# First half of the second layer's modulation moved to the head of the first layer's expert stage

## The chip, the cores and the metric

The kernel runs on one core of a Trainium2 chip. The metric is the device time of one execution in microseconds (us). Times below are counted from the start of the profiled span. The engines are TensorE (PE; PEld is its loading of weights), VectorE (DVE), ScalarE (ACT), GpSimd (POOL) and SyncE (SP). SyncE and GpSimd issue the transfers (DMAs); all of them run on the same 16 DMA engines, SyncE's in the queue that the profile calls q1 and GpSimd's in q0. An engine takes its instructions in the order in which they stand, and a wait holds up what is behind it.

## The reference

Two layers work on 1024 latent tokens and 256 context tokens, each of width 1024 in float32. A layer mixes tokens (two convolutions, windowed and global attention), then runs 16 experts of which each takes its best 128 latent tokens (and 32 context tokens, in the first layer only). Both parts are modulated by a vector that comes from the conditioning `c` alone:

```
mods = silu(c) @ ada_w[i] + ada_b[i]                 # 6 x 1024 values: sh1, sc1, g1, sh2, sc2, g2
h = rms_norm(x, n1) * (1 + sc1) + sh1                # input of the mixers
x_new = x + g1 * (mixers(h) @ w_out)
h2 = rms_norm(x_new, n2) * (1 + sc2) + sh2           # input of the experts
x_new = x_new + g2 * expert_choice_ffn(h2, ...)
# expert_choice_ffn: gates, idx = top_k(softmax(h2 @ router)); rows h2[idx];
# y = (silu(rows @ w_gate) * (rows @ w_up)) @ w_down; added back to rows idx with the gates
```

`ada_w[i]` is 1024 x 6144. It depends on no token, so layer 2's modulation can be computed at any time before layer 2.

## The kernel before

**Precision.** Every large product is made of three matmuls (`mm3`, L272 to L274) on a high and a low part of both sides. Weights are split as they arrive: ScalarE rounds a half chunk to its high part `wh` (L110), VectorE subtracts to get the low part `wl` (L111). There are five `wh` and five `wl` buffers in the first layer's expert stage.

**The expert stage (`moe`).** For each expert, gate, up and down weights come as four chunks of 128 x 4 x 512 floats (1 MiB, tile `rw`, L1188). The chunks go through a ring of 11 buffers (`raw`, made of two pools of 6 and 5), strictly in turn: a chunk that is asked for earlier takes the earlier buffer, whoever asks. The rows of an expert are gathered by an indirect transfer (`xs`, L1262), transposed on TensorE (`pt`, L1250) and split; gate and up products go to `pm`, their product is transposed, multiplied by down weights, scaled by the gate values and the modulation row `g2b`, and scattered with addition into `xacc` (L1343). The context's share of an expert is small matmuls straight from `rw` (L1235); a chunk's buffer is free once both have read it.

**The head of the stage.** The projection before it ends with the router's logits; `topk_x` finds the 128 best tokens of all 16 experts on VectorE (L1115 to L1118), turns the table over on TensorE (L1132, L1134) and writes `idx` (L1141). The gather of expert 0 needs `idx`. While the top-k runs, SyncE already asks for expert 0's weights: the four gate chunks and two up chunks. The other two up chunks and three gate chunks of expert 1 are issued by GpSimd, behind the gathers.

**The modulation.** One modulation step (`ada_mm`, L168) loads one 1 MiB chunk of `ada_w` into the same ring (`rw`, L171) and makes 16 small matmuls with the conditioning as the stationary side (`pc` from `rw` and `cT`, L174). `ada0(l, ...)` is the first third of the modulation (sh1 and sc1) in eight steps. After the fourth and the eighth it adds the bias tile `abias` (`mt`, L190), transposes the sum on TensorE (two transposes, L193) and writes `modT` (L196, L198). The bias tile is first cleared by VectorE (L160) and then filled by two small transfers (L165). `ada(l, 1, ...)` is the second third (g1 and sh2), eight steps again, then one addition and a store to `mods` (L211, L216). `moe` chains the two generators for layer 2 into `nxt`, and `pump(nxt, n)` runs `n` steps of it. Before the change the only places are one step in each of experts 1 to 10 and whatever is left (six steps) after the loop. So "first half" in the title is the eight steps of `ada0`. The last third (`raw`, L171) is made in layer 2's front.

**Order.** The program is written in this order, and a scheduler then moves instructions within their dependences; the order on each engine is fixed before the kernel runs.

Of the kernel before, what the change touches and what calls it, by code (L numbers as in the profile page):

```python
# [51 lines left out]
class Trunk:  # L52
# [1091 lines left out]
    def moe(self, l):  # L1144
# [6 lines left out]
        with ExitStack() as st:  # L1151
# [108 lines left out]
            def fetch(e):  # L1260
                xs = wk.tile([128, D], F32, name="xs")
                self.ga_mark = nc.gpsimd.indirect_dma_start(out=xs, out_offset=None, in_=self.h2[l],  # L1262
                                             in_offset=bass.IndirectOffsetOnAxis(ap=idx[:, e:e + 1], axis=0))
                return xs, fetch_c(e) if CTX and e else None

            def fetch_c(e):
                xc = wc.tile([64, 512], F32, name="xc")
                nc.gpsimd.indirect_dma_start(out=xc, out_offset=None, in_=hv,
                                             in_offset=bass.IndirectOffsetOnAxis(ap=idc[:, e:e + 1], axis=0))
                return xc  # L1270
# [81 lines left out]
            nxt = iter(())  # L1352
            if l + 1 < self.layers:
                stage = (raw.tile([128, 4, 512], F32, name="rw", tag="raw") for _ in itertools.count())
                nxt = itertools.chain(self.ada0(l + 1, stage, mp, _Renamed(psc), pst),
                                      self.ada(l + 1, 1, stage, 4, mp, _Renamed(psc)))
            last, xg = l + 1 == self.layers, None
            x = fetch(0)
            ga0 = self.ga_mark
            X = gather(0, x)  # L1360
# [148 lines left out]
```

## Time and profile before

| what | value |
|---|---|
| median of 3 runs | 2796.9 us (2791.25 to 2802.22) |
| the profiled execution, its own time | 2792.68 us |
| its span | 2790.9 us |
| TensorE busy in the span | 2564.8 us, 92% |
| VectorE, ScalarE, GpSimd busy | 2073.6, 1553.0 and 397.9 us |
| moved from and to memory | 594.44 MB, 213 GB/s on average |
| granted clock of TensorE over the span | 0.968 of full speed |
| top-k at the head of the first expert stage | 704.75 to 742.2 us |
| first matmul of expert 0 | 749.72 us |

The profiled execution is 4.2 us below the median. A row of the trace has the start, the duration, the engine, the line of the kernel, the operation and its tiles, and in brackets how long the engine sat idle before it and what ended that.

### The profile page before, as it was taken

The page shows a single profiled execution, that of the slowest core. Times are in us where ns is not written, and L with a number is a line of the kernel's source. Part 1 is how long each engine was busy: PE and PEld are TensorE (multiplying, and loading weights), DVE is VectorE, ACT ScalarE, POOL GpSimd, SP SyncE. Part 2 cuts the span into 40 slices and gives each one's busy share as a digit, 9 for nine tenths or more (in the row PEclk, how much of TensorE's full clock was granted, in tenths as well). Part 3 has the DMA queues.
Part 4 walks back from the last instruction along what each step waited for, and adds up shares of the span by engine and source line. Part 5 has one row for each costly group of instructions (what it writes and reads, how often), then busy time and mean ns, then how long its engine had stood idle before and what let it go on. Part 6 is the DMA issues. An engine that isn't in the chain of part 4 may idle for free.

```text
span 2790.9 us, 44135 instructions
## 1 busy us (share of the span) xinstructions
PE 2564.8 (92%) x17043; PEld 2033.0 (73%) x17043; DVE 2073.6 (74%) x3076; ACT 1553.0 (56%) x2255; POOL 397.9 (14%) x713
## 2 busy tenths in 40 slices
PE   6999988999799999999998899989996699999994
PEld 5898777877566666666665699777875588887783
DVE  4368866765877777777775558776766899989896
ACT  5212366743366666666664622466632588887774
POOL 1152000000520111111100142100001011111111
PEclk8999999999899999999999899999998899999998
DMA  6345100133689898989886442300048699999995
GB/s 239 115 133 179 57 9 16 33 113 127 240 294 318 295 318 290 330 289 326 276 302 225 135 146 79 98 9 9 9 171 297 249 369 377 377 376 377 376 339 203
DMA packets 297819, 594.44 MB, mean 213 GB/s; under 512 B 20446, under 2 KB 47560, under 8 KB 297608
## 3 DMA queue, kind: packets, MB, share of 16 engines
q1 hardware_dynamic: 275288, 515.58, 52.1%
q0 software_dynamic: 22320, 76.03, 9.0%
q8 instruction: 134, 2.20, 0.3%
q14 instruction: 77, 0.63, 0.1%
HBM read 541.16 MB, written 50.40 MB: 212 GB/s over the span
## 4 chain that ended last, share of the span: by engine, by line
PE 74%; issue 9%; DVE 6%; DMA 5%; ACT 4%; POOL 1%; SPq 0%; POOLq 0%; ACTq 0%; DVEq 0%
PE pm L273 10%; PE pm L272 10%; PE pm L274 10%; PE mm L272 6%; PE mm L274 5%; PE mm L273 5%; PE pc L1235 4%; PE pb L881 4%; PE po L272 2%; PE po L273 2%; PE po L274 2%; PE pb L864 2%; PE pt L1250 2%; PE Sx L793 1%; PE Sl L793 1%
## 5 line engine op out<-in xcount | busy, mean ns | idle before, releaser
L111 DVE TENSOR_TENSOR wl<-rw,wh 128x1024 fp32r<-128x1024 f32 x762 | 908.6, 1220 | 126.3 <-ACT wh L110 102.6
L110 ACT ACTIVATE wh<-rw 128x1024 fp32r<-128x1024 f32 x762 | 794.6, 1059 | 230.8 <-PE pm L274 186.8
L273 PE MATMUL pm<-wl,xh 128*128 128x512 f32 x1024 | 410.4, 401 | 3.4 <-DVE wl L111 2.3
L274 PE MATMUL pm<-wh,xl 128*128 128x512 f32 x1024 | 400.2, 391 | 0.0
L272 PE MATMUL pm<-wh,xh 128*128 128x512 f32 x1024 | 399.7, 395 | 0.0
L272 PEld LDWEIGHTS pm<-wh,xh 128*128 128x128 f32 x1024 | 193.1, 189 | 54.2 <-issue 12.6
L273 PEld LDWEIGHTS pm<-wl,xh 128*128 128x128 f32 x1024 | 192.9, 188 | 51.1 <-DVE wl L111 9.1
L274 PEld LDWEIGHTS pm<-wh,xl 128*128 128x128 f32 x1024 | 193.0, 188 | 37.4
L272 PE MATMUL pm<-wh,hh 128*128 128x512 f32 x512 | 202.0, 397 | 9.5 <-ACT wh L110 9.5
L273 PE MATMUL pm<-wl,hh 128*128 128x512 f32 x512 | 203.9, 398 | 6.3 <-DVE wl L111 6.3
L274 PE MATMUL pm<-wh,hl 128*128 128x512 f32 x512 | 201.7, 394 | 0.0
L1343 POOL DMA_INDIRECT xacc<-y,idx x31 | 86.8, 2799 | 647.2 <-DVE y L1330 647.2
L548 DVE SCALAR_TENSOR_TENSOR yab<-u,pT,yab 128x1295 f32<-128x1295 f32 (+1 forms) x120 | 166.4, 1419 | 0.2
L272 PE MATMUL mm<-wh,hh 128*128 128x256 f32 x512 | 145.7, 286 | 4.3 <-ACT cd L456 3.6
L273 PE MATMUL mm<-wl,hh 128*128 128x256 f32 x512 | 144.0, 282 | 0.0
L274 PE MATMUL mm<-wh,hl 128*128 128x256 f32 x512 | 143.9, 281 | 0.0
L274 PE MATMUL mm<-hh,wl 128*128 128x512 f32 x320 | 126.0, 399 | 0.0
L273 PE MATMUL mm<-hl,wh 128*128 128x512 f32 x320 | 125.5, 398 | 0.0
L272 PE MATMUL mm<-hh,wh 128*128 128x512 f32 x320 | 124.9, 406 | 0.0
L110 ACT ACTIVATE wh<-wr 128x512 fp32r<-128x512 f32 x72 | 45.1, 628 | 141.8 <-DMA wr<-in_w_in_dram 71.8
L272 PEld LDWEIGHTS pm<-wh,hh 128*128 128x128 f32 x512 | 96.6, 189 | 29.9 <-ACT wh L110 10.5
L273 PEld LDWEIGHTS pm<-wl,hh 128*128 128x128 f32 x512 | 96.6, 189 | 29.4 <-DVE wl L111 10.2
(406 smaller groups left out, 5172.4 us busy)
## 6 DMA issues: line engine op xcount, KB each, us to landing
rw<-in_w_down_dram SPq DMA_DIRECT2D x127, 1024.0 KB
rw<-in_w_up_dram SPq DMA_DIRECT2D x125, 1024.0 KB
rw<-in_w_gate_dram SPq DMA_DIRECT2D x123, 1024.0 KB
raw<-in_ada_w_dram SPq DMA_DIRECT2D x48, 512.0 KB
wr<-in_w_in_dram SPq DMA_DIRECT2D x72, 256.0 KB
rw<-in_ada_w_dram SPq DMA_DIRECT2D x16, 1024.0 KB
xt<-in_x_dram SPq DMA_DIRECT2D x16, 512.0 KB
wr<-in_w_out_dram SPq DMA_DIRECT2D x16, 512.0 KB
```

Of the source, the lines that this page charges most:

```text
L110: a = self.nc.scalar.activation(hi, src, AF.Copy)
L111: self.mark = self.nc.vector.tensor_sub(lo, src, hi.bitcast(F32))
L272: nc.tensor.matmul(p, lh, rh, start=first, stop=False)
L273: nc.tensor.matmul(p, lh, rl, start=False, stop=False)
L274: self.pe_mark = nc.tensor.matmul(p, ll, rh, start=False, stop=last)
L548: nc.vector.scalar_tensor_tensor(o, x, pT[:, b, k:k + 1], o, op0=OP.mult, op1=OP.add)
L793: nc.tensor.matmul(o, q[:, qs], K[:, kv, k0:k0 + n], start=i == 0, stop=i == 1 and not more)
L864: nc.tensor.transpose(p[:, j], Ps[hh][:, i * 128:i * 128 + 128], self.idn)
L881: nc.tensor.matmul(po[64 * hh:64 * hh + 64, z, 0], V[:, b, kv * 64:kv * 64 + 64], u.PT[:, hh * nk + i], start=i == 0, stop=i == nk - 1)
L1235: nc.tensor.matmul(pc[32 * j:32 * j + 32], xcT[:, kk * 4 + k, :], rt[2 * h + kk][:, k], start=k == 0, stop=k == 3)
L1250: nc.tensor.transpose(p[:, j], src[:, (4 * b + j) * 128:(4 * b + j + 1) * 128], self.idn)
L1343: nc.gpsimd.indirect_dma_start(out=acc, out_offset=bass.IndirectOffsetOnAxis(ap=idx[:, e:e + 1], axis=0), in_=y, in_offset=None, compute_o ...
```

## The change

`nxt` is pumped by eight steps before expert 0's rows are fetched: all of `ada0` for layer 2. The loop of experts is untouched, so the one step in each of experts 1 to 10 now belongs to the second third: experts 1 to 8 have its eight steps, expert 9 its addition and store, and nothing is left for expert 10 or for the call after the loop.

```
--- before.py
+++ after.py
@@ -1355,6 +1355,7 @@
                 nxt = itertools.chain(self.ada0(l + 1, stage, mp, _Renamed(psc), pst),
                                       self.ada(l + 1, 1, stage, 4, mp, _Renamed(psc)))
             last, xg = l + 1 == self.layers, None
+            self.pump(nxt, 8)
             x = fetch(0)
             ga0 = self.ga_mark
             X = gather(0, x)
```

The generators and the pump themselves:

```
def ada_mm(self, l, n, k0, kn, rt, p):
    nc.sync.dma_start(rt, w[k0 * 128:(k0 + kn) * 128, n * 512:n * 512 + 512]...)
    for k in range(kn):
        for j in range(4):
            nc.tensor.matmul(p[32 * j:32 * j + 32], self.cT[:, k0 + k], rt[:, k, j * 128:j * 128 + 128], ...)
def pump(self, gen, n):
    for _ in range(n):
        if next(gen, None) is None:
            return
```

How the built order changes at the two places:

SyncE at the head of the first layer's expert stage (a piece of the difference; `rw` are the ring's chunks, `abias` the bias tile):

```order
 L985 DMA xt<-in_ctx_dram 128x1024 x2
+L171 DMA rw<-in_ada_w_dram 128x4x512 x8
 L1188 DMA rw<-in_w_gate_dram 128x4x512 x4
 L1188 DMA rw<-in_w_up_dram 128x4x512 x2
 L1167 DMA g2b<-mods_65 128x1024
 L1174 DMA cg_8099<-mods_65 32x512 x2
-L165 DMA abias<-in_ada_b_dram 4x4x128 x2
+L165 DMA abias<-in_ada_b_dram 4x4x128 x4
```

All eight modulation chunks stand before the gate and up chunks of expert 0, and the bias that belongs to them stands behind those.

TensorE at the same place (a piece of the difference; `sm` and `mrg` belong to the index table, `xs` are the gathered rows, `mt` is the modulation sum with its bias):

```order
+L174 MATMUL pc<-rw,cT 32x128 x10
 L1134 MATMUL sm<-mrg,rev 128x16
-L1132 MATMUL sm<-idn,ixf 128x32
+L174 MATMUL pc<-rw,cT 32x128 x7
 L1134 MATMUL sm<-mrg,rev 128x16
+L174 MATMUL pc<-rw,cT 32x128 x50
+L193 MATMUL pt<-idn,mt 128x128 x4
 L1250 MATMUL pt<-idn,xs 128x128 x8
 L272 MATMUL pm<-wh,xh 128x512
```

The 128 modulation matmuls lie among the last steps of the index table, and the four transposes of `mt` stand before the transposes of expert 0's rows, where nothing stood before.

VectorE at the same place, after the change (`idx` is the index table, `wl` the low parts of the first gate chunks):

```order
L1141 TENSOR_TENSOR idx_79<-mg,sm 128x16
L111 TENSOR_TENSOR wl<-rw,wh 128x1024 x5
L160 MEMSET abias 128x512
L1115 MAX val_8381<-affc 16x8
L1118 MAX_INDEX ix_8382<-val_8381,affc 16x8
L190 TENSOR_TENSOR mt<-pc,abias 128x256
L196 COPY modT_69<-pt 128x4x2
L198 SCALAR_TENSOR_TENSOR modT_69<-pt,n1T 128x4 x2
L190 TENSOR_TENSOR mt<-pc,abias 128x256
```

The clearing of the bias tile, for which the bias transfers wait, stands behind the five subtractions of gate chunks; before, it stood ahead of `idx`, and the `mt` additions stood some experts later.

SyncE at the end of the first layer's expert stage, before the change (`xt` are tiles of the stream for layer 2):

```order
L1188 DMA rw<-in_w_down_dram 128x4x512 x4
L171 DMA rw<-in_ada_w_dram 128x4x512 x4
L514 DMA pr<-in_conv_b_w_dram 31x256
L515 DMA pr<-in_conv_b_b_dram 1x256
L516 DMA pr<-in_conv_ln_g_dram 1x256
L517 DMA pr<-in_conv_ln_b_dram 1x256
L518 DMA pr<-in_conv_a_w_dram 3x256
L171 DMA rw<-in_ada_w_dram 128x4x512 x2
L225 DMA xt<-xacc_71 128x1024 x4
```

After the change the two rows of `rw<-in_ada_w_dram` (six chunks) are gone from this place, and the rest stands in the same order.

## Rows read from the trace of the kernel before

**Rows 1.** Busy us per engine (instructions) in 720 to 740; then PEclk, DMA, GB/s.

```profile
720.00:740.00 20.00, 6.37 (x59) 4.00 (x57) 19.73 (x59) 9.31 (x13) 14.90 (x21) 0.72 0.94 343
```

**Rows 2.** Chain of waits, 740 to 760: start us, us, what.

```profile
741.64 1.00 DMA abias<-in_ada_b_dram
742.65 5.06 DMA xs<-h,idx
747.75 1.97 PE pt L1250 x8
```

**Rows 3.** SyncE's timeline at the head: start us, us, queue, line, operation, tiles.

```profile
693.22 0.38 SPq L1188 DMA_DIRECT2D rw<-in_w_gate_dram  x1
...
720.45 1.48 SPq L1188 DMA_DIRECT2D rw<-in_w_gate_dram  x3
```

**Rows 4.** TensorE's timeline at the seam, with the idle time before a row.

```profile
1500.40 1.08 PE L174 MATMUL pc<-rw,cT 128*32 128x128 f32 x32 [1.75 <-DMA rw<-in_ada_w_dram]
1503.11 1.08 PE L174 MATMUL pc<-rw,cT 128*32 128x128 f32 x32 [1.63 <-DMA rw<-in_ada_w_dram]
...
1505.70 0.84 PE L174 MATMUL pc<-rw,cT 128*32 128x128 f32 x18 [0.18 <-DMA rw<-in_ada_w_dram]
...
1532.82 1.08 PE L174 MATMUL pc<-rw,cT 128*32 128x128 f32 x32 [2.01 <-DMA rw<-in_ada_w_dram]
...
1542.65 1.35 PE L247 MATMUL pt<-idn,xt 128*128 128x128 f32 x4 [0.74 <-DVE xt L233]
```

**Rows 5.** Transfers by queue, 720 to 740: packets, MB, share of 16 engines.

```profile
q1 hardware_dynamic: 2804, 5.79, 80.4%
```

**Rows 6.** GpSimd's timeline behind the gathers of experts 0 and 1.

```profile
746.59 1.61 POOL L1188 DMA_DIRECT2D rw<-in_w_up_dram  x2
748.18 2.26 POOL L1188 DMA_DIRECT2D rw<-in_w_gate_dram  x3
```

**Rows 7.** Transfers by queue, 785 to 790, when both queues have work.

```profile
DMA packets 739, 1.97 MB, mean 394 GB/s; under 512 B 31, under 2 KB 31, under 8 KB 739
...
q0 software_dynamic: 270, 1.04, 53.6%
q1 hardware_dynamic: 469, 0.93, 49.8%
```

**Rows 8.** Splits (page, section 5); modulation by tile: ns min/median/max, first to last us.

```profile
L111 DVE TENSOR_TENSOR wl<-rw,wh 128x1024 fp32r<-128x1024 f32 x762 | 908.6, 1220 | 126.3 <-ACT wh L110 102.6
L110 ACT ACTIVATE wh<-rw 128x1024 fp32r<-128x1024 f32 x762 | 794.6, 1059 | 230.8 <-PE pm L274 186.8
...
L160 DVE MEMSET abias<- x6: 485/485/485, 1.3 to 1545.2; 128x512 f32 x6
...
L193 PE MATMUL pt<-idn,mt x8: 272/330/477, 24.8 to 1170.2; 128*128 128x128 f32 x8
...
L190 DVE TENSOR_TENSOR mt<-pc,abias x2: 409/409/409, 975.4 to 1169.5; 128x256 f32<-128x256 f32 x2
```

**Rows 9.** SyncE's timeline at the seam.

```profile
1522.25 1.15 SPq L171 DMA_DIRECT2D rw<-in_ada_w_dram  x2
1525.94 2.21 SPq L225 DMA_DIRECT2D xt<-xacc  x4
```

**Rows 10.** ScalarE's timeline at the seam: the last of four stream tiles.

```profile
1538.49 1.06 ACT L227 ACTIVATE junk<-xt 128x1024 bf16<-128x1024 f32 x1 [0.65 <-DMA xt<-xacc]
```

**Rows 11.** SyncE's timeline in the expert loop: the gate chunks, once per expert.

```profile
800.92 15.89 SPq L1188 DMA_DIRECT2D rw<-in_w_gate_dram  x4
...
944.36 15.35 SPq L1188 DMA_DIRECT2D rw<-in_w_gate_dram  x4
...
994.28 15.80 SPq L1188 DMA_DIRECT2D rw<-in_w_gate_dram  x4
...
1283.76 16.21 SPq L1188 DMA_DIRECT2D rw<-in_w_gate_dram  x4
...
1424.84 16.29 SPq L1188 DMA_DIRECT2D rw<-in_w_gate_dram  x4
```

More of the change, by code (lines that the diff above doesn't have):

```diff
@@ L1357, in moe @@
             last, xg = l + 1 == self.layers, None
+            self.pump(nxt, 8)
             x = fetch(0)
```

## The prediction, made before the changed kernel was run

> **What bounds the kernel now.** I read the chain of waits first, then the stretches between 720 and 840 us, then the queues' own rows, and last the seam between the layers at 1,495 to 1,540 us. Inside the expert loop TensorE sets the pace. At the head of the stage it does not: from 720 to 740 us it is busy for 6.37 of 20 us while VectorE works through the top-k for 19.73, and the transfer engines are at 0.94 of their time [rows 1]. That last number matters most for this change: TensorE is free there, the transfer queue is not. The head ends with the index table, the gather of expert 0 (742.65, 5.06 us) and the eight transposes of the gathered rows, 747.75 to 749.72 [rows 2]. What SyncE loads until then is six chunks of 1 MiB: one buffer is free at 693.22, the next only from 720.45 [rows 3], when the output projection gives its space back. The seam is bound by what the first matmuls of layer 2 need: the last scatter, and four loads of the stream behind it.
>
> **The change, part by part.** Sixteen steps of layer 2's modulation (1 MiB of weights and 16 small matmuls each) stood one in each of experts 1 to 10 and six behind the loop. Now eight stand ahead of everything in the stage, eight in experts 1 to 8, and none behind it.
>
> *The head.* The eight steps are 128 matmuls; 16 of them take 1.08 us at most [rows 4], so 8.6 us, beside 13.6 us in which TensorE idles between 720 and 740 [rows 1]. On TensorE alone they would cost nothing. Three orders make them cost something. On TensorE the four transposes of `mt` stand before the eight of the gathered rows. `mt` needs the bias tile, and its clearing stands on VectorE behind five subtractions on the first three gate chunks. And the bias transfer then stands in SyncE's queue behind all that was issued before.
>
> So when does the bias land? SyncE's queue from 720.45: seven modulation chunks (the eighth, first in order, goes at 693.22), four gate and two up chunks, 13 x 1.0486 = 13.63 MB, the broadcast gate row 0.52 and two small ones 0.13, together 14.28 MB. From 720 to 740 that queue moved 5.79 MB in the profiled run [rows 5], with the same buffers free at the same times, so 8.49 MB are left at 740. GpSimd's queue has, from then, one 0.52 MB write of the context rows, two gathers of 0.52 and five late chunks of 1.05: 6.81 MB, the five late ones issued from 746.59 to 750.44 [rows 6]. Where both queues have work they share evenly: 1.04 and 0.93 MB in 785 to 790, 394 GB/s together [rows 7]. With even shares GpSimd's five chunks need 5.24 / 0.197 = 26.6 us from 750, nearly as long as SyncE's, so all 15.3 MB pass before the bias: 38.8 us, to 778.8. The bias itself takes 1.0 us when nothing is ahead of it [rows 2]. Then, twice, one addition of 0.41 and two transposes of 0.33 [rows 8], with copies between: 2.4 us. The transposes of the gathered rows start at 782.2 and not at 747.75: **+34.4 us**. The chunks of gate and up are in place by then, so the first expert runs as before from there; the five splits that wait for gate chunk three (1.06 and 1.22 each [rows 8]) end well before the bias lands.
>
> Its bounds: if SyncE's queue were served first, 8.49 MB and the 1.57 MB of gathers and context rows that come before the late chunks would be through at 740 + 10.06 / 0.394 = 765.5, which gives 768.9 and +21. If the bias did not have to wait its turn, the third gate chunk would decide: two modulation and three gate chunks less the 0.55 MB already moved, 4.7 MB, are left at 740 to its end; 2.0 of them pass by 749 beside the gathers and the rest at half the rate, so it lands at about 763; then 1.06 + 1.22, the clearing 0.49 [rows 8], about 2 for the issue and the transfer and 2.4 for the chain: 770, +22. Above: the 343 GB/s of [rows 1] for the whole in place of 394 is 6 us more, +40. I take +34, the case that the row of two queues shows.
>
> The Trainium skill, "DMA: Bandwidth & Descriptors", section "Queues, rings and completion order", says that each engine goes round between the queue rows that have work, packet by packet. By that the two queues have equal shares and the sum is +34, as [rows 7] has it; it speaks against the +21, and against this change. The same section says that completion is not first-in, first-out for one issuing engine, since a small copy may run on fewer rings than a large one. By that alone the bias could land early and the head would be the +22. The trace speaks for the queue's order: at the seam SyncE issues four stream loads at 1525.94, behind two modulation chunks of 1522.25 [rows 9]; the second of these is used at 1532.82 [rows 4], and the last stream tile only at 1538.49 [rows 10].
>
> *The experts.* From 1283.76 to 1424.84 there are three experts without a step: 47.03 us each. From 800.92 to 1283.76 there are ten with one: 482.84 - 470.3 = 12.5 us for ten steps. The two that close a half of the modulation (944.36 to 994.28 is one, 49.92 us) cost 2.9 more than an expert without a step [rows 11]; the other eight 0.84 each. Afterwards there are eight plain ones, 6.7 us: **-5.8 us**. Bounds: -1.7 (two plain steps less) and -12.5 (none shows).
>
> *The seam.* Before the last expert's down product TensorE waits 1.75 and 1.63 us for modulation chunks and computes two steps of 1.08 [rows 4], 5.5 us, of which about 1.3 would be needed anyway until the split of the transposed rows is done: 4.2. Two more steps lie among the down matmuls, 2.1 us in all (0.84 of it in the row at 1505.70). Then the scatter goes 6.2 us sooner. Behind it the stream loads no longer stand behind two chunks: 2.1 MB / 0.394 = 5.3 us. **-11.5 us**. What is late next there is the normalisation of the four stream tiles, as now. Bounds: -5 if the loads of the context stream or of the projection weights, which keep their place behind the context's scatter, take the place of the stream tiles, and -14.
>
> Sum: 34.4 - 5.8 - 11.5 = **+17 us**. The profiled execution took 2792.7 us, so 2809.8; the median of the runs shown is 4.2 us above it (2796.9), and the prediction is set against that: 2814.
>
> **The rivals.** (1) *SyncE's queue is served first*, or the late chunks of GpSimd start late: +21 - 17 = +4, 2801. For it: the late chunks also wait for modulation matmuls now. Against it: the even shares of [rows 7]. (2) *The bias overtakes*: +22 - 17 = +5, 2802. For it: it is two transfers of 8 KB. Against it the order of [rows 4, 9, 10]. (3) *The head stays hidden*, the point of the move: had the bias landed before the gather's rows are there (747.7), nothing would be paid at the head and 17 us gained, 2780. The place is TensorE's four `mt` transposes; it decides this way only if SyncE's queue is empty by about 744, and 8.49 MB at 740 say that it is not. (4) *Slower still*: the head at its upper bound and the seam at its lower, 40 - 5.8 - 5 = +29, 2826, if layer 2's first weights, not the stream, are what its first matmuls wait for.
>
> **How the numbers follow.** The forecast has 0.66, (1) 0.16, (2) 0.08, (3) 0.03, (4) 0.07. A measurement of this kernel can tell about 0.5%, 14 us, from no change. The forecast's own range is +11 to +24, so about 0.77 of it is above 14: 0.51; with (4) and a little of (1) slower has 0.59. Within 0.5% are the rest of the forecast and nearly all of (1) and (2): 0.37. Faster: (3) and a corner of (2), 0.04. The range leaves out (3) and the outer ends: +2 to +30 about 2797, 2799 to 2827.
>
> **What would show it.** Right: TensorE nearly idle from about 735 to 780 but for the 128 matmuls, with the wait of the `mt` addition put down to the bias transfer; both queues busy to the end of it; the first `pm` matmul at about 784; SyncE's issues for later experts some 28 us later at expert 11 than now; the first transposes of layer 2 only some 17 us later than 1542.65. Wrong: a first `pm` matmul before 772 (then the shares or the order of the queue are not what I took); a bias that lands while the up chunks are still moving; experts without a step that are not 47 us; or a seam that gives back under 5 us. If the first `pm` matmul is at 784 and the time is still within 10 us of before, it is the seam that I took too small.

## The result: 2814.2 us after, 2796.8 us before

On one chip, run in turn, the changed kernel took 2814.2 us (median of four, 2809.1 to 2816.4) and the kernel before 2796.8 us (2791.3 to 2802.2): a ratio of 1.0056, 95% interval 1.0040 to 1.0072. It is slower by 17 us; 2814 was forecast. The profiled executions differ by 16.4 us in their spans (2807.3 and 2790.9), and that difference can be followed through the trace. (1.8 us of it lie ahead of the stage: SyncE's first load there is issued at 695.04, at 693.22 in [rows 3].)

| point of the program | before | after | later by | foreseen |
|---|---|---|---|---|
| transposes of expert 0's gathered rows | 747.75 | 784.61 | 36.9 | 34.4 |
| expert 0's down loads issued | 780.83 | 811.53 | 30.7 | |
| gate loads of expert 2 issued | 800.92 | 835.80 | 34.9 | 34.4 |
| gate loads ten experts on | 1283.76 | 1315.19 | 31.4 | 28.6 |
| last gate loads | 1424.84 | 1455.99 | 31.2 | 28.6 |
| scatter of the last expert's latent rows | 1519.73 | 1543.88 | 24.2 | 22.4 |
| first transposes of layer 2 | 1542.65 | 1562.98 | 20.3 | 17.1 |
| end of the span | 2790.9 | 2807.3 | 16.4 | 17.1 |

The same stretch as in [rows 1], and the one behind it up to the landing of the bias (columns as in [rows 1]):

```profile
720.00:740.00 20.00, 13.39 (x166) 10.14 (x165) 19.86 (x59) 5.85 (x9) 15.30 (x23) 0.78 0.85 309
748.00:784.00 36.00, 2.90 (x70) 2.20 (x62) 8.24 (x14) 5.06 (x5) 4.83 (x7) 0.59 0.96 358
```

TensorE takes the 128 small matmuls into its idle time of the top-k (13.4 us busy in place of 6.4) and then waits 32.4 us for `mt`, while the transfer engines are 0.96 busy. Which queue they serve, from 748 to 784 (packets, MB, share of 16 engines; q1 is SyncE's, q0 GpSimd's):

```profile
DMA packets 4903, 12.87 MB, mean 358 GB/s; under 512 B 266, under 2 KB 298, under 8 KB 4902
...
q1 hardware_dynamic: 3254, 6.56, 49.8%
q0 software_dynamic: 1648, 6.29, 45.7%
```

Over the 36 us the two queues move about the same, but not side by side: until 752 SyncE's queue is nearly alone (1.41 of 1.56 MB from 748), and from 776 on it is alone. Where both have work, from 752 to 776, it is this:

```profile
q0 software_dynamic: 1596, 6.12, 66.7%
q1 hardware_dynamic: 1604, 3.19, 36.4%
```

The shares are even in packets and two to one in bytes, since a packet of GpSimd's queue holds 3.8 KB here and one of SyncE's 2.0. [rows 7] is a mixture too: from 786 to 788, with both at work, it was 128 and 134 packets, 0.52 and 0.27 MB. The Trainium skill, on the page "DMA: Bandwidth & Descriptors", section "Queues, rings and completion order", says that each engine goes round between the queue rows that have work, packet by packet. The trace agrees with 1596 against 1604 packets; even shares of the bytes, as the prediction took them, do not follow from it and were not there.

The chain of waits across it (start us, us, what), where [rows 2] stood before:

```profile
751.60 20.92 DMA rw<-in_w_gate_dram
...
774.26 7.82 DMA abias<-in_ada_b_dram
782.17 0.44 DVE mt L190
782.65 0.70 PE pt L193 x2
...
784.82 1.71 PE pt L1250 x8
786.52 0.67 PE pm L272
```

The bias lands at 782.1, the `mt` transposes follow, and behind them the transposes of the gathered rows, in the order that the program has on TensorE. The timelines of the engines, for the rest of the table ([rows 3, 9 to 11] before):

```profile
695.04 41.06 SPq L171 DMA_DIRECT2D rw<-in_ada_w_dram  x8
773.61 12.20 SPq L165 DMA_DIRECT2D abias<-in_ada_b_dram  x4
785.07 0.07 DVE L1117 MATCH_VALUE_LOAD affn<-val,affc 16x8 f32 x1
...
811.53 7.97 SPq L1188 DMA_DIRECT2D rw<-in_w_down_dram  x4
835.80 16.36 SPq L1188 DMA_DIRECT2D rw<-in_w_gate_dram  x4
...
1221.49 16.20 SPq L1188 DMA_DIRECT2D rw<-in_w_gate_dram  x4
1455.99 16.37 SPq L1188 DMA_DIRECT2D rw<-in_w_gate_dram  x4
...
1543.88 1.57 POOL L1343 DMA_INDIRECT xacc<-y,idx  x1 [21.77 <-DVE y L1330]
1549.83 1.78 SPq L225 DMA_DIRECT2D xt<-xacc  x4
1557.64 1.06 ACT L227 ACTIVATE junk<-xt 128x1024 bf16<-128x1024 f32 x1
1562.98 2.67 PE L247 MATMUL pt<-idn,xt 128*128 128x128 f32 x8 [8.12 <-DVE xt L233]
```

One row there was not in the forecast: at 785.07 VectorE goes on with the context's top-k (`affn`), which had begun at 769.07 and stopped. Experiment e1 shows what it waited for.

### The profile page after: what moved, and what is told of

Its sections match the earlier page's. It is cut to its first block, busy times and chain, and to the rows that moved or that the text cites. A ratio compares the mean times of both kernels' runs of the same rounds, so it can differ in the third digit from the quotient of the medians.

```text
span 2807.3 us, 44132 instructions
## 1 busy us (share of the span) xinstructions
PE 2569.6 (92%) x17043; PEld 2036.2 (73%) x17043; DVE 2074.4 (74%) x3076; ACT 1552.5 (55%) x2255; POOL 387.3 (14%) x713
## 4 chain that ended last, share of the span: by engine, by line
PE 56%; issue 23%; DVE 6%; DMA 6%; ACT 5%; POOL 3%; SPq 1%; POOLq 0%; ACTq 0%; DVEq 0%
PE pm L273 6%; PE pm L272 6%; PE pm L274 6%; PE mm L272 6%; PE mm L273 5%; PE mm L274 5%; PE pb L881 3%; PE po L272 2%; PE po L273 2%; PE po L274 2%; PE pb L864 2%; DMA rw<-in_w_gate_dram 1%; PE Sx L793 1%; PE Sl L793 1%; PE pt L1250 1%
## 5 line engine op out<-in xcount | busy, mean ns | idle before, releaser
L272 PEld LDWEIGHTS pm<-wh,hh 128*128 128x128 f32 x512 | 96.6, 189 | 32.1 <-ACT wh L110 10.6
```

What stands on the lines that cost most here:

```text
L272: nc.tensor.matmul(p, lh, rh, start=first, stop=False)
```

## The experiments

Twelve kernels, each timed in five rounds or more against the kernel before on the same chip. The first eight are on the head, the others on the experts and the seam. For comparison, the changed kernel is at 1.0056. As executions reach the stage at slightly different times, the head's price is read in each as the time from SyncE's first load of the stage to the gate loads of expert 2, less the 107.7 us (800.92 - 693.22) of the kernel before:

| kernel | at the head | first load | gate loads | head's price | ratio |
|---|---|---|---|---|---|
| changed | 8 steps | 695.04 | 835.80 | 33.1 | 1.0056 |
| e9 | 8, bias on its own queue | 696.67 | 831.50 | 27.1 | 1.0039 |
| e2 | 8, bias there | 697.35 | 829.47 | 24.4 | 1.0051 |
| e4 | 4 | 695.83 | 818.02 | 14.5 | 1.0025 |
| e1 | 8, closing later | 696.52 | 846.33 | 42.1 | 1.0084 |
| e5 | e1, own scratch | 698.46 | 829.10 | 22.9 | 1.0024 |
| e6 | 8, own scratch | 697.06 | 839.10 | 34.3 | 1.0058 |
| e11 | 8, only bytes left | 697.82 | 826.04 | 20.5 | 1.0030 |
| e12 | 4, bias there | 697.08 | 810.11 | 5.3 | 0.9975 |
| e3 | none | 696.74 | 807.52 | 3.1 | 0.9965 |

(In e3 the issue of two modulation chunks in place of one, 3.43 us in place of 0.39, stands ahead of the gate loads and makes up its 3.1. Two kernels further down bear the measure out: e10, with the changed kernel's head, has 33.1, and e8, with the head of before, -0.1.)

### e9: the bias on a queue of its own

```diff
-            nc.sync.dma_start(bias[r:r + 97:32], src)
+            (q or nc.sync).dma_start(bias[r:r + 97:32], src)     # q = nc.scalar for layer 2's first half
```

> The changed kernel with one edit: the two bias transfers of the first half (8 KB each) are issued by ScalarE, on a queue that nothing else uses, and not by SyncE behind 14 MB. All loads, matmuls and the order on TensorE and VectorE stay; the clearing of the bias tile on VectorE still stands behind five subtractions on the first three gate chunks and ends at about 769. Theory (the place in SyncE's queue): the bias lands 2 to 4 us after its issue, at about 773 in place of 782, mt's transposes follow at 773.5, those of the gathered rows at about 775.5 in place of 784.6, and the time is 8 to 10 us below the changed kernel, 2805. Rival: whatever queue it is in, a transfer issued at 770 ends only when the engines have worked off what was issued before (about 782); then nothing changes, 2813 to 2815.

Measured: 2807.0 us, ratio 1.0039 (1.0026 to 1.0053).

SyncE in the changed kernel, then three rows of e9:

```profile
758.53 12.49 SPq L1167 DMA_DIRECT2D g2b<-mods  x1
...
770.90 1.72 ACTq L165 DMA_DIRECT2D abias<-in_ada_b_dram  x2
778.47 0.42 DVE L191 TENSOR_TENSOR mt<-pc,abias 128x256 f32<-128x256 f32 x1 [6.81 <-DMA abias<-in_ada_b_dram]
780.91 1.92 PE L1251 MATMUL pt<-idn,xs 128*128 128x128 f32 x8
```

The direction is right, the size two thirds: counted from the stage's first load the gathered rows come 5.3 us sooner, not 9, and the head is 6.0 us cheaper. Between two full queues 16 KB took 7.6 us from issue to use, where I had put 2 to 4; in the changed kernel it was 8.6 (773.61 to 782.17). So only 1.0 of the 5.3 us is a faster passage. The other 4.3 are an earlier issue: in the changed kernel the clearing is done at 769.1, but SyncE is held by the issue of the `g2b` load until 771.0 and issues the bias at 773.61, while ScalarE issues it as soon as the tile is clear. Being behind SyncE's other loads is worth some 6 us, and the clearing behind the third gate chunk comes next.

### e2: no bias to wait for

```diff
-        bias = self.ada_bias(l, 0, sp)
+        bias = self.ada_bias(l, 0, sp) if l == 0 else None       # layer 2: bT, transposed at the program's start
...
-                nc.vector.tensor_add(mt[:, :2], p[:, :2], bias[:, hf:hf + 3:2])
+                nc.vector.tensor_copy(mt[:, :2], p[:, :2])       # bT is added to the transposed result
```

> The bias of the first half is loaded and transposed at the start of the program and added behind the mt transposes, so no bias load and no clearing stand between the matmuls of the eight steps and the mt transposes; their order on TensorE (ahead of those of the gathered rows) stays. On VectorE the copy into mt still stands behind five subtractions on the first three gate chunks. Theory: the wait that ends last is then the third gate chunk, which lands at 766.3 in the changed kernel: mt at about 769, transposes of the gathered rows at about 771, first gate product at about 773 in place of 786.5: 13 us less, 2801. Rival A (bytes ahead of expert 0's weights): no gain from this either, 2812 or more, with the wait moved to the weights of the up product. Rival C: with the bias there the head is wholly hidden, first gate product before 757, 2785 or less.

Measured: 2809.2 us, ratio 1.0051 (1.0037 to 1.0064), an interval that holds the changed kernel's ratio too.

```profile
770.72 0.69 PE L201 MATMUL pt<-idn,mt 128*128 128x128 f32 x2 [18.09 <-DVE mt L198]
...
777.76 0.20 PE L1116 MATMUL pc<-idn,iv 16*64 16x16 f32 x1 [4.61 <-DVE iv L1114]
...
777.94 1.97 PE L1263 MATMUL pt<-idn,xs 128*128 128x128 f32 x8
```

`mt` is where the third gate chunk puts it (769 expected, 770.7 seen). But in this build the two small transposes of the context's top-k (`iv`) stand ahead of the gathered rows on TensorE, and these come at 777.9, not 771. The head is 8.7 us cheaper, and of that little is seen in the ratio (0.0005, 1.4 us); where the rest was lost is not shown.

### e4: half the bytes ahead

```diff
-            self.pump(nxt, 8)
+            self.pump(nxt, 4)
...
-                if 1 <= e < 11:
+                if 1 <= e < 13:
```

> Four steps at the head in place of eight, and twelve in experts 1 to 12 (none behind the loop, as in the changed kernel). The bias keeps its place at the end of SyncE's queue, with 4.2 MB less ahead of it. Theory: both queues are then empty 4.2 MB / 394 GB/s = 10.6 us sooner, so the bias lands at about 771.5, the first gate product is at about 776 in place of 786.5, four more steps in the experts cost 5 us, and the time is some 5 to 6 us below the changed kernel: 2808. Rival: what is paid at the head is a fixed cost of the order on TensorE and VectorE, not the bytes: first gate product at 784 or later, 2818.

Measured: 2802.4 us, ratio 1.0025 (1.0016 to 1.0034).

```profile
763.93 0.42 DVE L190 TENSOR_TENSOR mt<-pc,abias 128x256 f32<-128x256 f32 x1 [11.43 <-DMA abias<-in_ada_b_dram]
...
764.89 1.92 PE L1250 MATMUL pt<-idn,xs 128*128 128x128 f32 x8
```

The price goes with the bytes, not with a fixed order, and faster than expected: the gathered rows come 19.7 us sooner for 4.2 MB, 213 GB/s. (One of the two closings went from the head with them; it is about 1.5 us in the changed kernel, 782.17 to 783.68.) The expectation let the bias wait until both queues are empty. In e4 only SyncE's is, at about 763, while GpSimd's goes on. What stands ahead of the bias in its own queue passes at a third of the rate while the other queue has work (0.58 of 1.60 MB from 752 to 756 in e4), so 4.2 MB cost nearly 20 us and not 10.6. Half as many steps cost less than half as much at the head (14.5 against 33.1).

### e1: the closing in expert 1

```diff
+                    if i + k0 == 5:
+                        nc.vector.tensor_copy(mt[:, 2 * hf:2 * hf + 2], p[:, :2])
                     yield 0
+        bias = self.ada_bias(l, 0, sp)      # from here on in expert 1
...
```

> The eight steps stay at the head with all their loads and matmuls; only their closing goes: the two halves of the modulation are copied as they are, and the bias load, the additions, the four mt transposes and the writes of modT come in expert 1 instead. Theory: the head costs what it does because the transposes of the gathered rows stand on TensorE behind the mt transposes, and these wait for a bias that stands at the end of SyncE's queue. Then the gathered rows are transposed at about 752, the first gate product goes at the pace at which its chunks land (the fourth at 772.5) and the up product at the pace of its own (the last at about 782), so expert 0 ends its up product at about 786 and not at 817, against 781 before: about 28 us less than the changed kernel, 2786, faster than before. Rival A: it is the 8.4 MB of modulation weights ahead of expert 0's own that cost the time, and the bias only marks their end: then expert 0 waits for its weights until the queues are empty and under 8 us come back, over 2806. Rival B: the matmuls among the top-k delay the index table and the gather: then the first transposes stay late and nothing comes back.

Measured: 2819.7 us, ratio 1.0084 (1.0070 to 1.0098): slower still, against every case that I had written down.

```profile
757.03 1.97 PE L1277 MATMUL pt<-idn,xs 128*128 128x128 f32 x8 [5.29 <-DMA xs<-h,idx]
...
806.99 0.08 DVE L1144 MATCH_VALUE_LOAD affn<-val,affc 16x8 f32 x1 [1.08 <-PE pt L220]
...
817.32 9.24 PE L1262 MATMUL pc<-rw,xcT 128*32 128x512 f32 x64 [0.47 <-ACT xcT L1208]
...
823.23 3.76 SPq L1215 DMA_DIRECT2D rw<-in_w_down_dram  x4
```

The gathered rows are transposed 27 us sooner, and the down loads are issued 12 us later. The context's top-k stands still until the `mt` transposes are through (`PE pt`): its scratch `affn` is allocated under the tag `mt`, with one buffer, so the two share it. The chain is: `mt` free, context's top-k, its gather, expert 0's context products at 817.3; these are the last to read the gate chunks, so only then are the ring's buffers free for the down weights. In the changed kernel the same chain hangs on the bias (785.07 above).

### e5 and e6: a scratch of its own

```diff
-        val, ix = self.topk(self.affc, NE, 32, wk, "mt")
+        val, ix = self.topk(self.affc, NE, 32, wk, "hl", aw)     # a buffer of another pool
```

e5 is e1 with this edit, e6 the changed kernel with it.

> The kernel of e1 (closing in expert 1) with one edit: the scratch of the context's top-k has a buffer of its own and no longer shares the one of mt. In e1 expert 0's gathered rows were transposed early (757.0), and yet the first down loads were issued at 823.2, later than the 811.5 of the changed kernel, since the context's top-k waited at 807.0 for the buffer that mt held, the context's products of expert 0 came at 817.3, and these free the buffers for the down loads. Theory (the shared buffer): without it the context's top-k ends by about 780, its products of expert 0 come at about 800, the down loads at about 803, and the time is 2800 to 2806, some 16 less than e1. Rival (the modulation's bytes ahead of expert 0's weights, as A before): the products of expert 0 wait for their weights anyway, no more than 4 come back, 2816 or more.

> The changed kernel with the same one edit (own scratch for the context's top-k), the closing at the head as there. Theory: in the changed kernel two things wait for the bias, the transposes of the gathered rows and, by the shared buffer, the context's top-k; the first sets the pace, since TensorE has the context's products of expert 0 some 23 to 29 us of products behind those transposes. So the context's top-k ends before 784, the first gate product stays at 786 and the time at 2811 to 2815. Rival: the context's chain sets the pace here too; then 8 us or more come back, below 2807.

Measured: e5 2802.6 us, ratio 1.0024 (1.0015 to 1.0033); e6 2813.2 us, 1.0058 (1.0045 to 1.0072). Both as the theory has it.

```profile
778.28 0.20 PE L1130 MATMUL pc<-idn,iv 16*64 16x16 f32 x1 [24.02 <-DVE iv L1128]
...
807.90 5.26 SPq L1215 DMA_DIRECT2D rw<-in_w_down_dram  x4
```

The edit takes 17 us from e1: the shared buffer is shown. In the changed kernel it takes nothing, since the gathered rows wait for the same bias.

### e11: only the bytes left

e2, and in addition on VectorE the copies into `mt` and the context's top-k ahead of the splits of the gate chunks:

```diff
+                with tc.issue_after(self.mt_mark.ins):
                     self.topk_c(mp, psc.tile([128, 512], F32, name="pc"))
...
-            with tc.issue_after(self.tk_mark.ins):
+            with tc.issue_after(self.tk_mark.ins), tc.issue_after(x_mark.ins) if CTX else nullcontext():
                 H = silu(0, X)
```

> The changed kernel's eight steps at the head and the same loads in the same order, but nothing else waits: the bias is there from the start of the program (as in e2), the copies into mt come ahead of the splits of the gate chunks on VectorE, the context's top-k ahead of them too (so the shared buffer is free early), and the split of the gathered rows ahead of the splits of the weights. What is left of the head is the modulation's 8.4 MB ahead of expert 0's weights. Theory: the gathered rows are transposed at about 755, the gate product goes at the pace of its chunks (third at 766, fourth at 772.5), the up product at that of its own (last at 782), the first down loads are issued at 788 to 795 in place of 811.5, and the time is 2790 to 2797: the bias, the order and the shared buffer were two thirds of the head's price. Rival A (bytes): the down loads are issued after 803 and the time stays over 2805.

Measured: 2805.2 us, ratio 1.0030 (1.0019 to 1.0041). The theory falls; the rival of the bytes holds, if narrowly (down loads issued at 804.3, over 803, and a time just over 2805).

```profile
768.18 1.06 ACT L111 ACTIVATE wh<-rw 128x1024 fp32r<-128x1024 f32 x1 [5.95 <-DMA rw<-in_w_gate_dram]
769.15 1.07 ACT L111 ACTIVATE xh<-pt 128x512 fp32r<-128x512 f32 x2
...
784.75 2.00 ACT L111 ACTIVATE wh<-rw 128x1024 fp32r<-128x1024 f32 x2 [3.81 <-DMA rw<-in_w_up_dram]
789.09 2.01 ACT L111 ACTIVATE wh<-rw 128x1024 fp32r<-128x1024 f32 x2 [2.34 <-DMA rw<-in_w_up_dram]
```

The gathered rows are transposed at 760.3, behind the two small transposes of the context's top-k. One order is left that was meant to go: on ScalarE the split of the gathered rows (`xh`) still stands behind the splits of the first three gate chunks, so the first gate product waits until 769.8. Then the splits wait for expert 0's up chunks, in place at 784.7 and 789.1. These are SyncE's two, which pass at a third of the rate (0.52 of 1.54 MB from 764 to 768) beside GpSimd's queue; GpSimd's own two had landed some 14 us after their issue at 752.5. The head's price is 20.5 us. So of the 33.1 in the changed kernel 13 are the bias and the orders that hang on it, and the 8.4 MB ahead of expert 0's weights are at most 20.5. GpSimd's queue holds three gate chunks of expert 1 at that time; whether sending those later would let the up chunks through was not tried.

### e12: four ahead, nothing waiting, two a piece

```diff
-            self.pump(nxt, 8)
+            self.pump(nxt, 4)                  # with e2's bias, copies into mt ahead of the splits
...
-                if 1 <= e < 11:
-                    self.pump(nxt, 1)
+                if 1 <= e < 7:
+                    self.pump(nxt, 2)
```

> Four steps at the head with the bias there from the start and the copy into mt ahead of the splits of the gate chunks; two steps in each of experts 1 to 6; none behind the loop. Theory: with 4.2 MB less ahead of them expert 0's weights are there in time and nothing at the head waits for the modulation, so the gathered rows are transposed at about 751 and the first gate product is at about 757 (753 in e3); the down loads are issued at about 788 (784.6 in e3); four steps less in the experts give 4 back: level with e3, 2784 to 2789, and some 15 below e4, which has the same four steps at the head behind the bias. Rival A (bytes): 4.2 MB at 394 GB/s are 10.6 us whatever else is done, 2794 to 2800.

Measured: 2788.4 us, ratio 0.9975 (0.9966 to 0.9984), within the theory's range. The gathered rows are transposed at 754.25, waiting for nothing but their own gather; the head's price is 5.3 us, of which 1 is the issue of a second chunk as in e3. Four steps at the head are almost hidden; eight were not in any arrangement tried.

### e3: no step at the head, two a piece

```diff
-            self.pump(nxt, 8)
...
-                if 1 <= e < 11:
-                    self.pump(nxt, 1)
+                if 1 <= e < 9:
+                    self.pump(nxt, 2)
```

> No step at the head; two steps in each of experts 1 to 8 instead, so that none is left behind the loop either. It has the changed kernel's seam and before's head. Theory (my terms as the two traces gave them): sixteen steps in the experts at 1.25 us each in place of ten, +7.5, and the seam gives back what it gave back in the changed kernel, 11 to 15 us: 4 to 8 us less than before, 2789 to 2793; the gate issue of expert 2 at about 801 as before, and experts with two steps at 49.5 us. Rival D: the seam had little to do with the six steps behind the loop, so that only the +7.5 shows: 2804. Rival E: the transfer engines, 0.90 busy in the loop with one more chunk per expert, become the bound when there are two: experts of over 51 us, 2810 or more.

Measured: 2786.5 us, ratio 0.9965 (0.9952 to 0.9979): faster than both kernels, and a little below what was expected.

```profile
807.52 13.47 SPq L1188 DMA_DIRECT2D rw<-in_w_gate_dram  x4
...
1519.72 1.57 POOL L1343 DMA_INDIRECT xacc<-y,idx  x1 [21.73 <-DVE y L1330]
```

From 807.52 to 1197.38 eight experts with two steps take 48.73 us each, against 46.93 in the four after 1244.15 that have none: 0.9 a step. The first of these gate loads is itself held back by the issue of two modulation chunks, so 0.9 is too little. The scatters of the experts' results have no such issue ahead of them. Those of experts 0 and 8:

```profile
817.09 2.35 POOL L1343 DMA_INDIRECT xacc<-y,idx  x1 [4.21 <-DVE y L1330]
...
1211.57 2.33 POOL L1343 DMA_INDIRECT xacc<-y,idx  x1 [27.14 <-DVE y L1330]
```

By them the eight experts take 49.3 us each, 1.2 a step; the same reading of the changed kernel, with one step a piece (849.58 to 1235.68), gives 1.3. From the last gate loads (1431.88) to the scatter of the last expert it is 87.84 us, as in the changed kernel, where it was 94.89 before.

### e10 and e8: steps put back behind the loop

```diff
-                if 1 <= e < 11:
+                if 1 <= e < 3:          # e10, with the eight steps at the head; six behind the loop
...
+                if 1 <= e < 15:         # e8, none at the head; two behind the loop
```

> The changed kernel's head (eight steps), but of the other eight only two in experts 1 and 2, and six behind the loop again, as in the kernel before. It puts a price on the seam alone. Theory: from the last gate issue to the scatter of the last expert it is 94.9 us as before and not 87.9 (+7), the stream loads stand behind two modulation chunks again (+3 to +5), and six steps fewer in the experts give 7.5 back: 2 to 5 us above the changed kernel, 2817 to 2819. Rival D (the seam gains from something other than the steps): the 87.9 stay, and the six steps less in the experts show alone: 2806 to 2808.

> No step at the head, one in each of experts 1 to 14, two behind the loop in place of six. Theory (the seam pays for the steps behind the loop): four more steps in the experts, +5, and two thirds of the 11 to 17 us that the seam gave back in the changed kernel and in e3, -7 to -11: 2790 to 2794. Rival D: the seam's gain came from something else than the steps, so that only +5 shows, 2800; or it needs the last step gone, 2797 to 2800.

Measured: e10 2819.1 us, ratio 1.0087 (1.0073 to 1.0101), as expected. e8 2800.3 us, 1.0019 (1.0010 to 1.0028), not as expected. SyncE's last gate loads and the scatter, in e10 and then in e8:

```profile
1449.62 16.29 SPq L1188 DMA_DIRECT2D rw<-in_w_gate_dram  x4
...
1546.65 1.57 POOL L1343 DMA_INDIRECT xacc<-y,idx  x1 [30.85 <-DVE y L1330]
```

```profile
1432.08 16.22 SPq L1188 DMA_DIRECT2D rw<-in_w_gate_dram  x4
...
1523.87 1.57 POOL L1343 DMA_INDIRECT xacc<-y,idx  x1 [25.16 <-DVE y L1330]
```

From gate to scatter: 97.0 us with six steps behind the loop (94.9 in the kernel before, which has six too), 91.8 with two, 87.9 and 87.8 with none. The seam pays for them, at 1.2 to 2 us each. The time of e8 is the 2800 of its rival D, but the rows are not: the seam did gain 3.1 of 7.0 us with four of the six steps gone. Counted from the stage's first load (696.31), its layer 2 begins 2.9 us sooner than before, at 1542.81. It lost that behind: its rotary tables are loaded 61.1 us after this, where it is 54.5 us in the kernel before and 50.1 in e3. The build placed the first tiles of layer 2 in another order; which row of it costs the 7 us was not tried.

### e7: four a piece

```diff
-            self.pump(nxt, 8)
...
+                if 1 <= e < 5:
+                    self.pump(nxt, 4)
```

> No step at the head, four in each of experts 1 to 4. Two in an expert cost 0.9 each (e3: eight experts at 48.73 against 46.94), one alone 1.25. Theory: what a step costs beside its matmuls is paid once per expert; four together cost 3.4 to 4 per expert, 14 to 16 in all, as e3 (14.3): 2784 to 2788. Rival E (transfer): 4.2 MB more in one expert's 48 us are 87 GB/s over 300, near the 394 that the queues reached, so weights come late: experts 1 to 4 of over 53 us, 2793 or more.

Measured: 2794.6 us, ratio 0.9990 (0.9981 to 0.9999): the rival. Experts with four steps and experts without (columns as in [rows 1]):

```profile
840.00:1030.00 190.00, 186.35 (x1356) 130.86 (x1360) 136.95 (x145) 115.89 (x135) 19.62 (x14) 0.98 0.98 342
1050.00:1230.00 180.00, 180.00 (x1006) 122.95 (x1005) 142.13 (x143) 121.72 (x140) 24.34 (x15) 1.00 0.86 291
```

The transfer engines are 0.98 busy and TensorE begins to wait. The scatters of experts 0 and 4:

```profile
817.10 2.36 POOL L1343 DMA_INDIRECT xacc<-y,idx  x1 [25.66 <-DVE y L1330]
...
1030.21 2.33 POOL L1343 DMA_INDIRECT xacc<-y,idx  x1 [3.15 <-DVE y L1330]
```

By these the four experts with steps take 53.3 us each: 1.6 us a step, where two a piece cost 1.2.

## Why the prediction was right, and where it was not

**The head.** Foreseen +34.4, measured +33.1 from the stage's first load to the gate loads of expert 2, and +36.9 at the gathered rows, 35.0 without the 1.8 us by which this execution came to the stage later. The bias landed at 782.1, where the sum has 779.8 (778.8 and 1.0 for the bias itself). SyncE's queue had moved 5.12 MB by 740 in place of the 5.79 of [rows 5]; the missing 0.67 MB are 1.7 us at 394 GB/s, which is the late start. The order in SyncE's queue and the place of the transposes on TensorE were as described.

Two rows were misread. The shares are even in packets, not in bytes: from 752 to 776 GpSimd's queue had 6.12 MB and SyncE's 3.19. That did not move the landing, as it rests on all bytes of both queues passing before the bias, whichever go first. But GpSimd's queue was empty some five us before the bias landed, where I had both busy to the end, and SyncE's chunks pass more slowly beside GpSimd's than I took them to (e4, e11). And the 1.0 us of [rows 2] is not the time of a bias transfer: in the kernel before, the bias was issued from 741.64 on and its 40 packets moved between 743.0 and 743.9. Rival (1) is ruled out by the queues' bytes, of which SyncE's had the smaller share, and rival (2) by the bias's own packets, 780.7 to 781.2, in the last two us of that queue; (4) needed a seam of 5 us, and it gave 10.8.

Two things about the head I did not see. The wait for the bias holds a second chain, by the buffer that `mt` shares with the context's top-k (e1, e5). And close behind the bias come the up chunks of expert 0: with no wait for the bias at all the head still costs 20.5 us (e11). Rival (3) was therefore priced wrongly, not only improbable: a bias that is there early would not have given -17, 2780, with eight steps; e2 and e11 gave 2809 and 2805. Most of the price goes with the bytes ahead of expert 0's weights: half of them less took 19 us from the head (e4), and from e11 to e12, where nothing waits for the bias, four steps less took 15. The bias was the last of these bytes.

**The experts.** Foreseen -5.8, measured -3.7 (34.9 to 31.2 in the table). The mis-sized term is the price of a plain step: I gave the two closing steps 2.9 us each and the other eight 0.84. In the changed kernel eight steps without such a closing cost (1221.49 - 835.80) / 8 = 48.21 us an expert against 46.9 without: 1.3 each. The mean of [rows 11], 1.25, was the better figure, and splitting it by one row of 49.92 us the error.

**The seam.** Foreseen -11.5: 6.2 to the scatter and 5.3 for the stream loads. Measured -7.0 and -3.8, in all -10.8. e10, e3 and e8 show the first part by itself. In the second the stream did gain what was foreseen: ScalarE comes to the last of the four tiles 13.8 us after the scatter (1557.64) in place of 18.8 [rows 10], 5.0 us sooner. Not all of it reached layer 2's first transposes, which now wait 8.1 us for the normalisation that I had named as what is late next.

**The sum.** By the first transposes of layer 2 the two executions are 20.3 us apart, not the 17 foreseen; the end is at +16.4 because layer 2 takes 3.9 us less between about 1703 and 1990, in its attention. Nothing in the change explains that. From the first transposes of layer 2 to the first matmul of its output projection it is 490.4 us before and 486.5 after; e6, e11 and e2, which differ from the changed kernel only ahead of the expert loop, have 486.9, 490.5 and 492.5. So kernels that are alike in this stretch differ there by as much; what makes it was not found. So the closeness of 2814 to 2814.2 is partly luck: the experts were taken 2 us too favourably, the execution came 1.8 us late to the stage, and an unexplained 3.9 us made up for both.

## What to carry to other kernels

Work that is free on an engine still brings its bytes. When a step is moved ahead of a stage's own loads, count what the queue carries until the stage's weights are in place, not only the wait that ends last today: here easing or removing that wait alone gave back 6 to 9 of 33 us (e9, e2), halving the bytes 19. The transfers had room inside the experts (0.86 busy where an expert has no step), and two steps in each of eight experts cost 1.2 us a step, beat both kernels (0.9965), and left the seam clean. Four in each of four were too many (0.98 busy, 1.6 a step).

Two queues with equal turns need not have equal bytes. Read the packets of each in a stretch in which both have work, and not a mean over one in which one of them rests.

A name shared by two tiles of one buffer is a wait between them. Before moving what fills one, look up who else is allocated under its tag.

## What the runs showed of the hardware that was not expected

Beside two queues at work, a small transfer is slow even on a queue of its own. In e9 two transfers of 8 KB were issued from 770.9 on, their 40 packets moved between 775.1 and 777.8, and the addition that waits for them began at 778.47. With next to nothing beside them, in the kernel before, the 40 packets of the same kind of load moved within 0.9 us, 743.0 to 743.9, from 1.4 us after the issue. The Trainium skill, "DMA: Bandwidth & Descriptors", section "Rules for kernel authors", says that spreading transfers over issuing engines does not help bandwidth. The trace agrees: 385 GB/s from 770 to 779 in e9 with three queues, 386 in the changed kernel with two. What helped the small transfer was above all its issue, 4.3 us sooner.

The matmuls after the long idle stretch ran at a lower granted clock at first: 0.56 of full speed from 785 to 790, near the lower of the two levels (1.2 GHz, 0.50), and 1.00, 2.4 GHz, from 790 on. Before the change it was 0.52 from 748 to 753 and 1.00 after. So the longer idling cost nothing there that the idling beside the top-k had not cost already.
